# Feed-forward weights: two of the four block sums made by accumulating DMAs, the parts of seven blocks in one tile with five buffers

## The chip, the cores and the metric

One core of a Trainium2 chip runs the whole program: TensorE (PE in the profile; its weight loads PEld), VectorE (DVE), ScalarE (ACT), GpSimd (POOL), SyncE (SP), which issues DMAs, and 16 DMA engines. The metric is the time of one execution on the device in microseconds, the median of several runs.

## The reference, cut to what matters

Two layers of a transformer-like trunk on 640 tokens (512 latent, 128 context). Each layer has three token mixers, a merge with an output projection, and a SwiGLU feed-forward block. The change lies in the latter:

```python
D_MODEL = 1024
D_FF = 256 * ((8 * D_MODEL + 3 * 256 - 1) // (3 * 256))      # 2816
...
    x = x + g1 * mix
    h = rms_norm(x, p['norm2']) * (1 + sc2) + sh2
    x = x + g2 * ((jax.nn.silu(h @ p['w_gate']) * (h @ p['w_up'])) @ p['w_down'])
```

Weights and activations are float32.

## The kernel before

A matrix product in float32 is made from float16 halves: `split` (L186 to L189) writes a rounded half on ACT and the remainder on DVE, and `mm3` (L192 to L202) multiplies high by high, low by high and high by low: three matmuls on each 128 x 128 weight tile.

The three feed-forward products are computed on 2 x 2 blocks with seven block products in place of eight, in the manner of Strassen and Winograd: the weight is cut in four blocks, the tokens in two halves of 320 (`HT`), and the depth in two. Each of the seven products needs one weight block or a sum of weight blocks, and one activation block or a sum of those.

`lhs_parts` (L1197 to L1217) prepares a chunk of weights: the DMA (L1203, issued on SP) loads four blocks of 128 x 256 (512 KB) to a raw tile `wf`, which has two buffers; three blocks are split as they are (`wh` and `wl`, or for every other chunk `uh` and `ul`); four sums go to the tile `ls` (L1210; three on POOL by `SUMP`, one on DVE), and these are split to `vh` and `vl`, four buffers. All of it is emitted at high priority. `block` (from L1219) runs the seven products on two chunks (or three rows of them at the end of the last group), copies some of the sums in PSUM out by ACT (`du`, `dp`) and adds others by DVE (`ff_o`, `ff_s`).

`ffn` (from L1268) runs eleven units u per layer. A unit (`gate_up`) is a block for the gate and one for the up weights, of two chunks each. `gate` takes tanh on ACT and a product on DVE; `up` multiplies in place on POOL, three of four quarters (L1307, tile `ff_s`). At the end of a unit `inputs` makes the block sums of the result (`rhs_sums`, L1189 to L1195, tile `ts`, on POOL but for the last unit) and splits them to the seven blocks of `f`. After units 0 to 4, 5 to 8 and 9 to 10 comes `down` with four blocks each. In layer 0 the modulation weights of layer 1 are loaded and multiplied in between. `norm_sums` (L1367) makes the seven activation blocks `xs` of the normed input, and also uses `rhs_sums`.

`wload` (L175) is the loader of the other weights. Its raw tile `wf` and halves `wh`, `wl` lie in the pool `wst`, which lives as long as the program and is shared with `lhs_parts`. Before the feed-forward comes `merge` (L1125), which also uses POOL (tile `mga`), and in which the first weight chunks of the feed-forward are prepared.

The order of instructions on each engine and each DMA queue is fixed when the program is built, by a scheduler that places them by a simulated time line and by priority. Every engine runs its instructions in that order, and an instruction that waits for a semaphore holds those behind it.

## Time and profile before

| | us |
|---|---|
| median of 3 runs | 2723.09 (2720.1 to 2725.29) |
| the profiled execution's own time | 2721.82 |
| its span, first to last instruction | 2719.8 |
| feed-forward of layer 0, about | 905 to 1385 |
| feed-forward of layer 1, about | 2245 to 2705 |

A busy time is the sum of an engine's instructions. Matmuls overlap in the pipeline, so that a busy PE need not run at its peak. "Idle before" is time in which an engine stood, with the instruction that ended the wait. The chain of waits is followed back from the last instruction: at each step to what released it, or to the instruction ahead of it on its engine. The mean granted clock of PE is 0.973 of its full 2.4 GHz.

### The profile page before, as it was taken

What the parts mean: (1) busy time and instruction counts of PE and PEld (TensorE: products, weight loads), DVE (VectorE), ACT (ScalarE), POOL (GpSimd) and SP (SyncE); (2) the same over time, 40 slices, a digit from 0 to 9 for tenths busy, and PEclk for the clock granted to TensorE, in tenths of its full rate; (3) what the DMA queues carried; (4) which work ended last, traced back from release to release, by engine and by line L of the source; (5) the groups of instructions that cost most, each with busy time, mean ns of one, the idle gap of its engine ahead of it and who ended that gap; (6) DMA issues with size and microseconds to landing.
All of it is one profiled execution on the core that took longest, in us unless ns stands there. A gap on an engine that the chain in (4) does not pass through costs nothing.

```text
span 2719.8 us, 52951 instructions
## 1 busy us (share of the span) xinstructions
PE 2495.5 (92%) x21022; PEld 1613.9 (59%) x21022; DVE 1810.2 (67%) x2966; ACT 1295.5 (48%) x2466; POOL 1093.1 (40%) x1012
## 2 busy tenths in 40 slices
PE   5999999999998899999889989999989988889896
PEld 3656666566345656656566666665653565656574
DVE  5749854325756778878787497442277657888887
ACT  5532754444642544444465346554545444444444
POOL 3252111111137567565533632011112565766764
PEclk9999999999998999999989999999999999999998
DMA  7787564436434164432243965543462621222222
GB/s 295 225 260 233 151 195 124 126 123 202 114 131 157 61 206 131 162 117 89 73 137 106 264 184 161 163 122 119 126 205 74 210 78 40 78 78 78 78 82 67
DMA packets 249400, 382.50 MB, mean 141 GB/s; under 512 B 109824, under 2 KB 155968, under 8 KB 249152
## 3 DMA queue, kind: packets, MB, share of 16 engines
q1 hardware_dynamic: 249152, 379.12, 45.0%
q8 instruction: 165, 2.70, 0.4%
q14 instruction: 83, 0.68, 0.1%
HBM read 291.30 MB, written 73.92 MB: 134 GB/s over the span
## 4 chain that ended last, share of the span: by engine, by line
PE 44%; DVE 18%; POOL 14%; DMA 12%; issue 5%; ACT 5%; SPq 2%; DVEq 0%; POOLq 0%; ACTq 0%
PE f L195 12%; PE g L195 8%; POOL ls L1210 8%; PE ao L872 5%; PE s L195 5%; DMA wf<-in_w_gu 3%; POOL ts L1191 3%; DMA wf<-in_w_down 2%; DVE wl L183 2%; POOL ff_s L1307 1%; DVE vl L189 1%; DVE wl L189 1%; DVE ul L189 1%; DVE z L671 1%; ACT wh L188 1%
## 5 line engine op out<-in xcount | busy, mean ns | idle before, releaser
L195 PEld LDWEIGHTS <-wh 128*128 128x128 f16 x5760 | 560.1, 99 | 250.8 <-issue 34.8
L195 PEld LDWEIGHTS <-wl 128*128 128x128 f16 x2880 | 285.6, 99 | 176.9 <-issue 70.8
L195 PE MATMUL s<-xs,vh 128*128 128x320 f16 x1408 | 308.2, 302 | 25.3 <-ACT du L213 10.7
L195 PEld LDWEIGHTS <-vh 128*128 128x128 f16 x2112 | 209.9, 100 | 92.1 <-issue 5.3
L195 PE MATMUL f<-hh,wh 128*128 128x320 f16 x896 | 251.1, 302 | 1.7 <-ACT st L213 1.6
L195 PE MATMUL f<-hh,wl 128*128 128x320 f16 x896 | 251.2, 301 | 0.0
L1210 POOL TENSOR_TENSOR ls<-wf 128x256 f32<-128x256 f32 (+1 forms) x136 | 137.3, 1014 | 203.7 <-DVE vl L189 188.4
L875 POOL TENSOR_TENSOR pacc<-pe,pacc 128x512 f32<-128x512 f32 x64 | 84.2, 1315 | 325.7 <-ACT pe L213 315.5
L195 PE MATMUL s<-xs,vl 128*128 128x320 f16 x704 | 203.9, 302 | 0.2 <-DVE vl L189 0.2
L195 PE MATMUL g<-hh,wh 128*128 128x320 f16 x704 | 198.7, 304 | 2.8 <-ACT sq L213 1.5
L195 PE MATMUL g<-hh,wl 128*128 128x320 f16 x704 | 198.4, 304 | 0.0
L189 DVE SCALAR_TENSOR_TENSOR vl<-ls,vh 128x1024 f16<-128x1024 f32 (+1 forms) x136 | 185.7, 1389 | 10.8 <-ACT vh L188 10.8
L329 DVE SCALAR_TENSOR_TENSOR wl<-wf,wh 128x512 f16<-128x512 f32 x130 | 89.1, 713 | 137.2 <-ACT wh L213 136.8
L195 PE MATMUL s<-f,vh 128*128 128x320 f16 x704 | 159.9, 310 | 17.1 <-ACT du L213 9.3
L195 PEld LDWEIGHTS <-vl 128*128 128x128 f16 x1056 | 104.8, 99 | 95.8 <-issue 49.2
L183 DVE SCALAR_TENSOR_TENSOR wl<-wf,wh 128x1024 f16<-128x1024 f32 (+4 forms) x116 | 132.6, 1157 | 33.3 <-ACT wh L182 33.0
L188 ACT ACTIVATE vh<-ls 128x1024 f16<-128x1024 f32 (+1 forms) x136 | 133.8, 1020 | 39.4 <-POOL ls L1210 39.3
L195 PE MATMUL f<-hl,wh 128*128 128x320 f16 x896 | 148.7, 299 | 0.0
L195 PE MATMUL s<-xs,wh 128*128 128x320 f16 x528 | 133.6, 306 | 10.0 <-ACT du L213 10.0
L814 POOL TENSOR_TENSOR rc<-rc,rot 128x512 f32<-128x512 f32 (+1 forms) x16 | 27.6, 1724 | 283.3 <-DVE rc L813 266.9
L182 ACT ACTIVATE wh<-wf 128x1024 f16<-128x1024 f32 (+4 forms) x116 | 95.2, 832 | 92.3 <-PE g L195 72.9
L195 PE MATMUL s<-xs,uh 128*128 128x320 f16 x528 | 134.4, 305 | 4.2 <-ACT uh L188 4.2
(382 smaller groups left out, 6202.1 us busy)
## 6 DMA issues: line engine op xcount, KB each, us to landing
wm<-in_w_mod SPq DMA_DIRECT2D x96, 512.0 KB, 4.6
wf<-in_w_gu SPq DMA_DIRECT2D x88, 512.0 KB, 3.6
wf<-in_w_in SPq DMA_DIRECT2D x112, 256.0 KB, 3.5
wf<-in_w_in SPq DMA_DIRECT2D x44, 512.0 KB, 4.0
wf<-in_w_down SPq DMA_DIRECT2D x40, 512.0 KB, 3.6
d_s<-sd SPq DMA_DIRECT2D x20, 768.0 KB, 5.4
d_gate<-st SPq DMA_DIRECT2D x96, 160.0 KB, 3.1
sd<-d_s SPq DMA_DIRECT2D x20, 768.0 KB, 5.7
```

The lines of the kernel that those rows point to most:

```text
L182: nc.scalar.activation(wh, wf, AF.Copy, scale=SW)
L183: nc.vector.scalar_tensor_tensor(wl, wf, SW, wh, op0=ALU.mult, op1=ALU.subtract)
L188: nc.scalar.activation(hi, src, AF.Copy, scale=scale)
L189: nc.vector.scalar_tensor_tensor(lo, src, scale, hi, op0=ALU.mult, op1=ALU.subtract)
L195: mm = lambda *a, **k: nc.tensor.matmul(out, *a, skip_group_check=more, **k)
L329: nc.vector.scalar_tensor_tensor(wl[:, sl], wf, SW, wh[:, sl], op0=ALU.mult, op1=ALU.subtract)
L671: nc.vector.tensor_tensor(z[a, j + 1:N, 0:cc], z[a, j + 1:N, 0:cc], wj, op=ALU.subtract)
L814: nc.gpsimd.tensor_tensor(w[:n], w[:n], self.rot[:n, NS:], op=ALU.mult)
L872: nc.tensor.matmul(po[64 * j:64 * j + 64, :], vt(h, kt), es[j], start=n == 0, stop=n == 4)
L875: nc.gpsimd.tensor_tensor(acc[1], es[1], acc[1], op=ALU.add)
L1191: sub = lambda i, x, y: (self.nc.gpsimd if i in pool else self.nc.vector).tensor_tensor(out[:, i], x, y, op=ALU.subtract)
L1210: tt = lambda i, x, y, op: (nc.gpsimd if i in SUMP else nc.vector).tensor_tensor(t[:, i], x, y, op=op)
```

## The change

The weights of a chunk now come as six blocks in HBM, in the order (1,1), (0,1), (0,0), (0,0), (1,1), (1,0) of the 2 x 2 blocks. SP loads the first five into the raw tile `wg` (640 KB, three buffers). A DMA issued on POOL then adds the sixth block to both of the last two, on their way into the tile (128 KB read as a broadcast, 256 KB written): these are two of the four sums. The third sum is made by DVE, the fourth by POOL, both in place in `wg`. The signs are chosen such that one row of the result comes out negative; that is put right in the scales of `gate`, of the f split, of `norm_sums` and of the modulation (a second `gscale`). The first three blocks are split as they are, the last four after the sums, all to one tile of seven blocks for each half (`pw0`, `pw1`, five buffers). The tables AT7 and BT7 say which slot holds the block of which product.

`rhs_sums` forms the activation sums with the signs that belong to it, in the order 0, 3, 1, 2, and the f split takes three of them together and the fourth by itself, where it was two and two. In `norm_sums` the fourth sum is split by itself too. The pools of `wload` are now opened for each layer: the halves (`wst`) are closed before the merge, the raw tiles (`wf`) before the feed-forward.

```diff
-NSUM = (2,)
+NSUM = (1,)
-SUMP = (0, 1, 3)
+AT7 = {4: 0, 2: 1, 1: 2, 3: 3, 6: 4, 7: 5, 5: 6}
+BT7 = {1: 0, 2: 1, 3: 2, 5: 3, 7: 4, 4: 5, 6: 6}
+WGB = 3
+PWB = 5
...
     def rhs_sums(self, out, b, pool=(0, 1, 2, 3)):
-        sub = lambda i, x, y: (self.nc.gpsimd if i in pool else self.nc.vector).tensor_tensor(out[:, i], x, y, op=ALU.subtract)
-        sub(0, b[:, 0], b[:, 1])
-        sub(1, b[:, 3], out[:, 0])
-        sub(2, b[:, 3], b[:, 0])
-        sub(3, b[:, 2], out[:, 1])
+        tt = lambda i, x, y, op: (self.nc.gpsimd if i in pool else self.nc.vector).tensor_tensor(out[:, i], x, y, op=op)
+        tt(0, b[:, 1], b[:, 0], ALU.subtract)
+        tt(3, b[:, 3], out[:, 0], ALU.add)
+        tt(1, b[:, 3], b[:, 0], ALU.subtract)
+        tt(2, out[:, 3], b[:, 2], ALU.subtract)
-    def lhs_parts(self, pool, src, n, c):
+    def lhs(self, pool, src, n):
+        tile = lambda tag, bufs, dt, q: self.sb(pool, [128, q * 256], tag, dt, bufs)[:, :q * 128 * n].rearrange("p (q x) -> p q x", q=q)
         with self.tc.high_priority():
-            a, t = wide(self.wp, "wf", F32, 2), wide(pool, "ls", F32, 2)
-            nc.sync.dma_start(a, src)
...
-            self.split(w[0], w[1], a[:, 1:4], SW)
-            tt = lambda i, x, y, op: (nc.gpsimd if i in SUMP else nc.vector).tensor_tensor(t[:, i], x, y, op=op)
-            tt(0, a[:, 0], a[:, 3], ALU.add)
-            tt(1, t[:, 0], a[:, 1], ALU.subtract)
-            tt(2, a[:, 1], a[:, 0], ALU.subtract)
-            tt(3, a[:, 2], t[:, 1], ALU.subtract)
-            self.split(v[0], v[1], t, SW)
+            a = tile("wg", WGB, F32, 5)
+            out = [tile(f"pw{i}", PWB, F16, 7) for i in range(2)]
+            nc.sync.dma_start(a, src[:, 0:5])
+            nc.gpsimd.dma_start(a[:, 3:5], src[:, 5:6].to_broadcast([128, 2, 128 * n]), accum_op=ALU.add)
+            self.split(out[0][:, 0:3], out[1][:, 0:3], a[:, 0:3], SW)
+            nc.vector.tensor_tensor(a[:, 2], a[:, 4], a[:, 2], op=ALU.add)
+            nc.gpsimd.tensor_tensor(a[:, 1], a[:, 2], a[:, 1], op=ALU.add)
+            self.split(out[0][:, 3:7], out[1][:, 3:7], a[:, 1:5], SW)
...
-                self.act(t, c, AF.Tanh, scale=0.5 * DS)
+                self.act(t, c, AF.Tanh, scale=(-0.5 if i > 1 else 0.5) * DS)
...
-            for a, b in ((0, 2), (2, 4)):
-                self.split(f[0][:, 3 + a:3 + b], f[1][:, 3 + a:3 + b], t[:, a:b], 0.5 * DS * DS * SF)
+            self.split(f[0][:, 3:6], f[1][:, 3:6], t[:, 0:3], 0.5 * DS * DS * SF)
+            self.split(f[0][:, 6], f[1][:, 6], t[:, 3], -0.5 * DS * DS * SF)
...
-                    parts(3, 7, ts)
+                    parts(3, 6, ts[:, 0:3])
+                    parts(6, 7, ts[:, 3:4], neg=True)
...
+        self.wp = self.pool(wfs, f"wf{l}", 2)
+        self.wq = self.pool(ws, f"wst{l}", 3)
...
+        ws.close()
         wr = self.pool(ys, f"wr{l}", 4, "right")
         self.modscale(l, 1)
         self.gscale(l, 16, DS)
         self.gscale(l, 40, 1.0 / (SW * SF))
+        self.gscale(l, 41, -1.0 / (SW * SF))
...
+        wfs.close()
         with ExitStack() as es:
             self.ffn(l, es, ExitStack())
```

## Rows read from the trace of the kernel before

**Rows 1.** The page: span, then busy time, share and instructions of each engine
```profile
span 2719.8 us, 52951 instructions
...
PE 2495.5 (92%) x21022; PEld 1613.9 (59%) x21022; DVE 1810.2 (67%) x2966; ACT 1295.5 (48%) x2466; POOL 1093.1 (40%) x1012
```

**Rows 2.** Windows: stretch, length, busy us per engine (instructions), granted clock, DMA share, GB/s
```profile
905.00:1385.00 480.00, 433.79 (x3246) 285.51 (x3243) 382.67 (x531) 213.74 (x356) 287.85 (x291) 0.97 0.39 127
2245.00:2705.00 460.00, 405.04 (x2822) 278.84 (x2820) 373.39 (x501) 207.60 (x346) 289.23 (x288) 0.96 0.22 68
...
2501.56:2529.84 28.28, 23.76 (x172) 16.53 (x170) 22.76 (x27) 12.92 (x21) 20.53 (x20) 1.00 0.23 75
...
2448.88:2460.47 11.59, 11.59 (x88) 8.32 (x87) 10.60 (x17) 5.40 (x9) 5.75 (x7) 1.00 0.32 93
```

**Rows 3.** Timeline of PE: start, length, engine, line, operation, count
```profile
2427.46 0.30 PE L195 MATMUL s<-f,vl 128*128 128x320 f16 x1
...
2428.28 0.30 PE L195 MATMUL s<-f,vl 128*128 128x320 f16 x1
```

**Rows 4.** Timeline of POOL in layer 0: first and last of four bursts ts
```profile
1151.76 3.52 POOL L1191 TENSOR_TENSOR ts<-ff_s 128x320 f32<-128x320 f32 x2
...
1242.02 3.54 POOL L1191 TENSOR_TENSOR ts<-ff_s 128x320 f32<-128x320 f32 x2
```

**Rows 5.** Chain of waits through one unit: start, length, what
```profile
2501.56 3.61 DMA wf<-in_w_gu
...
2508.43 1.72 POOL ff_s L1307
...
2510.22 1.78 POOL ts L1191 x2
...
2520.80 2.10 POOL ls L1210 x2
...
2522.92 4.75 DMA wf<-in_w_gu
...
2529.84 3.65 DMA wf<-in_w_down
```

**Rows 6.** Groups by shape, 2270 to 2690 us: busy us, mean ns, idle before
```profile
L189 DVE SCALAR_TENSOR_TENSOR vl<-ls,vh 128x1024 f16<-128x1024 f32 x59 | 81.4, 1398 | 2.7 <-ACT vh L188 2.7
...
L1210 POOL TENSOR_TENSOR ls<-wf 128x256 f32<-128x256 f32 x58 | 59.9, 1036 | 105.3 <-DVE vl L189 101.1 <-DMA wf<-in_w_down 3.1 <-DVE ls L1210 0.9
L188 ACT ACTIVATE vh<-ls 128x1024 f16<-128x1024 f32 x59 | 59.6, 1044 | 9.7 <-POOL ls L1210 9.6
L1210 POOL TENSOR_TENSOR ls<-ls,wf 128x256 f32<-128x256 f32 x58 | 57.3, 991 | 2.0
L1210 POOL TENSOR_TENSOR ls<-wf,ls 128x256 f32<-128x256 f32 x57 | 51.0, 900 | 2.0
...
L1210 DVE TENSOR_TENSOR ls<-wf 128x256 f32<-128x256 f32 x58 | 48.5, 858 | 0.3 <-DMA wf<-in_w_gu 0.2
```

**Rows 7.** The weight loads' line: issue time on SP, ns min/median/max
```profile
L1203 SPq DMA_DIRECT2D wf<-in_w_gu x88: 327/328/333, 821.1 to 2626.6; - x88
```

**Rows 8.** Tile ls over the span: ns min/median/max of the second split
```profile
L189 DVE SCALAR_TENSOR_TENSOR vl<-ls,vh x136: 678/1219/1892, 838.6 to 2695.5; 128x1024 f16<-128x1024 f32 x128, 128x512 f16<-128x512 f32 x8
```

**Rows 9.** DMA issues: count, KB each, median us to landing
```profile
wf<-in_w_gu SPq DMA_DIRECT2D x88, 512.0 KB, 3.6
...
sd<-d_kq SPq DMA_DIRECT2D x40, 256.0 KB, 5.2
...
wf<-in_w_down SPq DMA_DIRECT2D x8, 256.0 KB, 2.7
```

**Rows 10.** Timelines of SP and PE from layer 0 to layer 1
```profile
1368.64 0.89 SPq L181 DMA_DIRECT2D wf<-in_w_tm  x2
...
1382.31 0.30 PE L195 MATMUL s<-f,vh 128*128 128x320 f16 x1
...
1387.24 0.34 PE L195 MATMUL g<-wh,hh 128*128 128x192 f16 x2 [0.49 <-ACT hh L213]
```

More of the change, by code (lines that the diff above doesn't have):

```diff
@@ L136, in __init__ @@
         self.cp = pool("const", 1)
-        self.wp = pool("wst", 3)
         self.tp = pool("tmp", 2)
@@ L176, in wload @@
         nc = self.nc
[L177 to L179 removed]
+        wf = self.sb(raw, [128, n], "wf") if raw else self.sb(self.wp, [128, n], "wf")
+        wh = self.sb(pool or self.wq, [128, n], "wh", F16)
+        wl = self.sb(pool or self.wq, [128, n], "wl", F16)
         with self.tc.high_priority():
@@ L1216, in lhs_parts @@
-        pick = lambda x, q: [x[i][:, q] for i in range(2)]
-        return {1: pick(w, 0), 2: pick(w, 1), 4: pick(w, 2), 5: pick(v, 0), 6: pick(v, 1), 7: pick(v, 2), 3: pick(v, 3)}
+            a = tile("wg", WGB, F32, 5)
[3 more added lines that the diff above has]
+            self.split(out[0][:, 0:3], out[1][:, 0:3], a[:, 0:3], SW)
@@ L1219, in block @@
+            nc.vector.tensor_tensor(a[:, 2], a[:, 4], a[:, 2], op=ALU.add)
+            nc.gpsimd.tensor_tensor(a[:, 1], a[:, 2], a[:, 1], op=ALU.add)
+            self.split(out[0][:, 3:7], out[1][:, 3:7], a[:, 1:5], SW)
+        return {q: [[out[i][:, j, 128 * k:128 * k + 128] for k in range(n)] for i in range(2)] for q, j in AT7.items()}
     def block(self, pool, chunks, rhs, dst, done, urgent=False, after=None):
@@ L1312, in gate_up @@
                     next(mods, None)
-                chunks = [(self.lhs_parts(wp, self.a["w_gu"][l, u, g, c], 256, c), 2 * c, 2) for c in range(2)]
+                chunks = []
+                for c in range(2):
+                    chunks.append((self.lhs(wp, self.a["w_gu"][l, u, g, c], 2), 2 * c, 2))
                 blocks.append(self.block(fa, chunks, lambda q, i, k: xs[q][i][k], dst, done, after=(lambda: inputs(u, s)) if g else None))
@@ L1347, in down @@
                     n = min(2, us[-1] + 1 - u)
-                    src = self.a["w_down"][l, m // 2][:, 512 * u:512 * (u + n)].rearrange("p (q n) -> p q n", q=4)
-                    chunks.append((self.lhs_parts(wp, src, 128 * n, len(chunks)), u, n))
-                run(self.block(fa, chunks, lambda q, i, k: fs_[k][i][:, at7[q]], lambda i: self.sb(fa, [128, HT], "ff_o", bufs=3), done,
+                    chunks.append((self.lhs(wp, self.a["w_down"][l, m // 2][:, 768 * u:768 * (u + n)].rearrange("p (q x) -> p q x", q=6), n), u, n))
+                run(self.block(fa, chunks, lambda q, i, k: fs_[k][i][:, BT7[q]], lambda i: self.sb(fa, [128, HT], "ff_o", bufs=3), done,
                                last and m == KD - 2))
@@ L1387, in norm_sums, with parts @@
                             self.act(c, c, AF.Identity, scale=A, bias=sh)
-                def parts(a, b, src, eng=nc.vector):
+                def parts(a, b, src, eng=nc.vector, neg=False):
                     hi, lo = (xs[i][j][:, a:b, cs] for i in range(2))
-                    self.act(hi, src, AF.Copy)
-                    eng.tensor_tensor(lo, src, hi, op=ALU.subtract)
+                    if neg:
+                        self.split(hi, lo, src, -1.0)
+                    else:
+                        self.act(hi, src, AF.Copy)
+                        eng.tensor_tensor(lo, src, hi, op=ALU.subtract)
                 if h == 0:
@@ L1398, in norm_sums @@
                     parts(2, 3, nt[j][:, 3:4, cs], nc.gpsimd)
-                    parts(3, 7, ts)
-        return {q: [[xs[i][j][:, n] for j in range(4)] for i in range(2)] for n, q in enumerate((1, 2, 3, 5, 6, 7, 4))}
+                    parts(3, 6, ts[:, 0:3])
+                    parts(6, 7, ts[:, 3:4], neg=True)
+        return {q: [[xs[i][j][:, n] for j in range(4)] for i in range(2)] for q, n in BT7.items()}
     def final(self):
@@ L1576, in layout @@
     gu = gu.transpose(0, 7, 1, 3, 5, 6, 2, 4, 8)
-    quads = lambda w: np.stack([w[..., 1, 0, :, :], w[..., 0, 0, :, :], w[..., 0, 1, :, :], w[..., 1, 1, :, :]], -3)
-    r["w_gu"] = quads(gu).reshape(L, NF // 2, 2, 2, 128, 4, 256)
-    dn = f("w_down").reshape(L, 2, NF // 2, 128, 4, 2, 128).transpose(0, 4, 3, 5, 1, 2, 6)
-    dn = quads(dn)
+    six = lambda w: np.stack([w[..., i, j, :, :] for i, j in ((1, 1), (0, 1), (0, 0), (0, 0), (1, 1), (1, 0))], -3)
+    r["w_gu"] = six(gu).reshape(L, NF // 2, 2, 2, 128, 6, 256)
+    dn = six(f("w_down").reshape(L, 2, NF // 2, 128, 4, 2, 128).transpose(0, 4, 3, 5, 1, 2, 6))
     r["w_down"] = cat([dn[..., u:u + 2, :].reshape(L, 4, 128, -1) for u in range(0, NF // 2, 2)], -1)
```

16 lines of the change are left out of this document (3 added, 13 removed).

## The prediction

> **What bounds the kernel now.** I read the page first: PE is busy 92% of 2719.8 us [rows 1], which looks like a kernel bound by its matmuls. The table of windows says otherwise for the feed-forward stages, the only ones in which the change alters much. They run at about 905 to 1385 us (layer 0) and 2245 to 2705 us (layer 1), 940 us together [rows 2]. Matmuls there start about 0.136 us apart when nothing holds them: six steps lie between 2427.46 and 2428.28 [rows 3]. A block on two chunks is 7 products x 2 chunks x 2 x 3 = 84 matmuls, 11.4 us at that pace. One gate-and-up unit u is two blocks, so 22.9 us. The window of one unit is 28.28 us long and holds 172 matmul records; a block without the work at the end of a unit needs 11.59 us, nearly the pace of PE [rows 2]. So in each unit PE stands still for some 5.4 us, and blocks alone are fine. In layer 0, where the modulations of the next layer are mixed in, the three units between the sums at 1151.76 and 1242.02 take 30.1 us each [rows 4].
>
> Why a unit is late is in the chain of waits over that same window [rows 5]. It runs: a weight load, the split on ACT and DVE, the up product on POOL (ff_s), the sums ts, then the sums ls of the weights, which are queued among ff_s and ts, then the next load, which could not start before (a load issued at 2501.56, the next on the chain at 2522.92, the one after at 2529.84). The reason is the raw tile wf: it has two buffers, and the last reader is a POOL sum. A burst on POOL therefore holds the loads, and the split weights reach PE late. DVE is busy 22.76 of the 28.28 us and POOL 20.53 [rows 2], so neither is full, but DVE has little room: it would be the next bound at almost the time that PE needs.
>
> **What leaves POOL and what comes.** There are 136 chunks. Per chunk three POOL sums of 1.04, 0.99 and 0.90 us [rows 6] become one, so 1.95 us leave, 7.8 us in a unit of four chunks. In their place POOL issues one accumulating DMA per chunk. No DMA leaves POOL's queue in the trace of before, so its price there is unknown. Its lower bound is the 0.33 us that SP spends on an issue [rows 7], its upper one the 1.95 us which it replaces; I take 1.0, between the two, since an engine that computes must make the list of rows. Then POOL's work in a unit falls from 20.5 to 16.7 us. DVE keeps one sum (0.86 us) and both splits. It may gain: the second split takes 1.40 us on average in layer 1 and 1.22 at the median [rows 6, 8], and the long ones lie beside POOL's sums. I leave this out of the sum, as DVE does not decide a unit.
>
> **The new cycle of a raw buffer.** Three raw buffers wg replace two wf, and five tiles of parts (2.5 blocks) replace three plus two of wh/uh and four of vh. So the question is what time a wg buffer needs from one load to the next, divided by three.
> - Load: 256 KB land in 2.7 us and 512 KB in 3.6 [rows 9], 0.9 for each 256 KB, so 640 KB take 4.05.
> - Issue on POOL: 1.0.
> - The accumulating transfer writes 256 KB. Lower bound 2.7, a plain load of that size; upper bound 5.4, that load twice, as the destination is read too (the slow 256 KB row has 5.2 [rows 9]). I take 3.3, nearer to the plain load, because the broadcast source is only 128 KB. The first split lies beside it.
> - DVE sum 0.86, POOL sum 0.95, ACT 1.04, DVE 1.40 [rows 6].
>
> That is 12.6 us with no waiting. Now the waits. Before, a wf buffer needs 3.6 for the load and 3.8 for four sums, 7.4 us in all, but its cycle is half a unit, 14.1 us: 6.7 us of waiting in the queues. In a block without the burst it is 11.6, so 4.2. The new cycle is passed on by POOL twice, but POOL is lighter. I take 6 us with the burst and 4.4 without. The cycle is then 18.6 us, over three buffers 6.2 us per chunk and 24.8 us per unit; without the burst 17.0, so 11.3 per block, where PE's own 11.4 decides and nothing changes. A microsecond more or less in the cycle is worth 1.33 us per unit.
>
> So a unit falls from 28.3 to 24.8 us. Ten units per layer (the first is prepared during the merge) give 35 us in layer 1. In layer 0 I take 3.0 us per unit, as the modulation's matmuls fill part of its 30.1 us: 30 us. Together 65 us.
>
> **The other edits.**
> - norm_sums: the last split becomes two on ACT and two on DVE, 8 times per layer. The extra DVE operation is smaller than the 0.86 us sum [rows 6]; all 16 on the path would be 13.7 us, none 0. I take 3, as that stretch waits in turn on ACT, DVE and POOL.
> - The raw and half tiles of wload now live per layer, and the next layer's lie where the f tiles were. Today layer 1's first loads are issued at 1368.64 while the feed-forward ends, and the first product of that layer runs at 1387.24 [rows 10]. If they must wait for the last product on f (about 1382), a load of 2.7 to 3.6 us and its split come later: between 0 and 6 us, once; I take 3.
> - SP: the same number of loads, each a quarter larger. Behind a load that waits for its buffer on SP stand the next weights, in layer 0 the loads of the modulations, and the stores d_x at the end. They wait today in the same way.
> - POOL: the issue waits for its load to land. Behind it are ts, ff_s, the sum of the next chunk and, in the merge, mga; the splits of f on ACT and the second split wait for those. POOL's idle 7.8 us of a unit cover it; what it costs without is the first rival.
> - rhs_sums has as many sums. The f split now needs all four sums first; f is read only by the later down blocks, which hide this, except at the last unit, where one split, about a microsecond, could show. In the merge two sums leave POOL for an issue, which about cancels. The turned signs ride on scales that exist, and one small DVE scale per layer is new: nothing.
>
> **Sum.** The profiled execution took 2721.8 us. Minus 65, plus 6, gives 2662.8; the median of the runs shown is 2723.1, 1.3 above it, so 2664.
>
> **The rivals.**
> POOL's queue blocks (slower). If the scheduler puts an issue right behind its load in time, POOL stands up to the whole 4.05 us and everything behind it too. POOL then needs 16.7 + 4 x 4.05 = 32.9 us per unit, 4.6 more than 28.3; 20 units give 92. A block without burst has 5.75 us of POOL work [rows 2], less 3.9 plus 2.0 plus 8.1 is 12.0 against 11.6, another 10 over 24 blocks. With the 6 us of the other edits the time is 2721.8 + 108 + 1.3, about 2831. It decides from a mean wait of 2.9 us, (28.3 - 16.7) / 4. For: four waits per unit on an engine that runs in order. Against: today POOL's sums follow the same loads and wait little.
>
> The round trip is too long (slower). Its point is a cycle of 21.2 us (28.3 x 3 / 4), so an issue and transfer of 6.9 us together with my waits. If the transfer reads twice over, in two passes of 5.2 us [rows 9], the cycle is 18.6 - 3.3 + 10.4 = 25.7, a unit 34.3 us: 20 x 6.0 = 120, and blocks without burst 16.1 against 11.6, 24 x 4.5 = 108; some 2957. At the milder 5.4 us the unit is 27.6 us and the blocks 12.7, and the sum comes out about 2741. The Trainium skill, in "Collectives: The Full Stack" (The bandwidth ceiling), says that an add inside a DMA is slow because it reads two sources, which halves the rate, not because of the adding. By it the transfer would be at my upper bound of 5.4; no row of before shows an add in a DMA.
>
> PE decides (faster still): with the short bounds (0.33 and 2.7) the cycle is 17.3, 23.1 us per unit, almost PE's 22.9. Then 52 in layer 1 and 45 in layer 0: 2632.
>
> Nothing is gained: the burst ff_s, ts stays in front of the second split's sum, or DVE at 22.8 us keeps its order, and a unit stays at 28. Time 2715 to 2730. For: POOL still stands twice in the cycle. Against: raw and split weights for four blocks can be in store in place of three, and the burst takes POOL less than one block's time.
>
> **How the numbers follow.** Forecast 0.42 (2640 to 2700), PE decides 0.14, nothing gained 0.12, POOL blocked 0.19, long trip 0.13. A measurement tells 0.2%, 5.4 us, from no change. Faster 0.42 + 0.14 + 0.04 of "nothing" = 0.60; same 0.08; slower 0.32. Both signs hold much, so the range reaches from 2610, below the PE case by its unknowns, into the blocked and long cases up to 2790, leaving about 0.04 below and 0.14 above; the likeliest case alone has 2640 to 2700.
>
> **What would show it.** A unit in layer 1 (distance between ts bursts) near 25 us, blocks without burst at 11.4 to 11.7; POOL issues of about 1 us; 256 KB accumulating in 3 to 4 us; POOL waiting for wg under 2 us each. Wrong: POOL waits for wg of 3 us or more (first rival), splits on ACT waiting for the accumulated tile with POOL idle (second), or a unit still near 28 with DVE idle for POOL (fourth).

## The result and the profile after

The changed kernel takes 2750.35 us (2745.9 to 2755.07), the kernel before on the same chip 2724.19 us. The ratio is 1.0098, 95% interval 1.0074 to 1.0122: 1% slower, where I forecast 2664. Its profiled execution took 2747.1 us, 2745.2 of them span.

The page of the changed kernel, first its engines (as [rows 1]) and its software queue, then three groups and three DMA issues with their landings (as [rows 6] and [rows 9]):

```profile
PE 2503.0 (91%) x21022; PEld 1606.3 (59%) x21022; DVE 1739.1 (63%) x2984; ACT 1308.2 (48%) x2482; POOL 941.4 (34%) x876
...
q0 software_dynamic: 36992, 34.61, 8.8%
...
L192 ACT ACTIVATE pw<-wg 128x1024 f16<-128x1024 f32 (+3 forms) x272 | 247.7, 923 | 251.4 <-POOL wg L1213 157.7
...
L1210 POOL DMA_DIRECT2D wg<-in_w_gu x88 | 105.6, 1205 | 218.9 <-DMA wg<-in_w_gu 120.3
...
L1212 DVE TENSOR_TENSOR wg<-wg 128x256 f32<-128x256 f32 (+1 forms) x136 | 91.8, 680 | 87.6 <-DMA wg<-in_w_gu 61.5
...
wg<-in_w_gu SPq DMA_DIRECT2D x88, 640.0 KB, 4.9
...
wg<-in_w_down SPq DMA_DIRECT2D x40, 640.0 KB, 4.1
...
wg<-in_w_gu POOLq DMA_DIRECT2D x88, 256.0 KB, 4.6
```

POOL lost 152 us of work, as meant, and DVE 71. But POOL now stands for its load before an issue, DVE for the accumulating transfer before its sum, and ACT for POOL before the second split. Windows of two units in layer 1 (as [rows 2]; their ends are the starts of ts bursts):

```profile
2514.62:2542.88 28.26, 24.48 (x164) 16.16 (x163) 18.64 (x26) 13.22 (x20) 15.31 (x15) 0.94 0.56 131
2542.88:2571.70 28.82, 25.94 (x185) 17.31 (x183) 23.14 (x29) 13.65 (x22) 16.86 (x16) 1.00 0.58 129
```

A unit is as long as before, 28.3 and 28.8 us (28.3 in [rows 2]). POOL has 15 to 17 us of work in it instead of 20.5 and the DMA engines are busy 0.56 to 0.58 of the time instead of 0.23. The chain of waits through the first of these units (start, length, what), to be laid beside [rows 5]:

```profile
2521.18 4.90 DMA wg<-in_w_gu
...
2526.64 4.37 DMA wg<-in_w_gu
...
2531.10 0.06 DVE wg L1212
...
2531.93 1.55 DVE pw L193
...
2535.04 5.10 DMA wg<-in_w_gu
...
2540.71 1.20 POOL wg L1210
```

Before, POOL's sums of weights stood between two loads. Now two transfers stand there, one behind the other: a load of 4.90 us and then, from 2526.64, the accumulating transfer of 4.37.

Where the 25.4 us of the span went is read from the first and last matmul of each stage, from the start of one to the start of the other, in one execution of each kernel. In us; "L1 mixers" are the products on hh, the merge runs from the first product on the mixers' results (yh) to the last one with w_out, FFN are the products on xs and f; the kernels are those of the experiments below:

| kernel | L0 merge | L0 FFN | L1 mixers | L1 merge | L1 FFN | span |
|---|---|---|---|---|---|---|
| before | 123.6 | 468.6 | 580.8 | 122.2 | 453.6 | 2719.8 |
| after | 129.2 | 470.5 | 589.3 | 128.9 | 447.5 | 2745.2 |
| e1_no_acc | 120.7 | 440.6 | 590.7 | 121.0 | 411.5 | 2659.1 |
| e3_pool_waits | 121.2 | 440.7 | 593.3 | 120.8 | 414.4 | 2672.1 |
| e2_plain | 123.2 | 456.0 | 589.9 | 123.9 | 436.2 | 2705.0 |
| e13_two_loads | 129.1 | 457.0 | 585.2 | 127.6 | 429.9 | 2712.5 |
| e17_other_order | 122.3 | 474.4 | 585.1 | 125.5 | 453.3 | 2735.4 |
| e8_engine_sums | 125.4 | 468.4 | 590.7 | 125.5 | 449.5 | 2737.2 |
| e4_wgb4 | 127.9 | 471.9 | 581.4 | 127.0 | 446.3 | 2734.4 |
| e4c_wgb4_pwb5 | 111.0 | 457.7 | 577.7 | 110.0 | 438.4 | 2718.3 |
| e11_behind | 109.8 | 453.6 | 588.0 | 109.3 | 439.6 | 2723.1 |
| e5_pools | 124.2 | 469.3 | 584.2 | 124.1 | 456.5 | 2733.6 |
| e6_late | 124.2 | 469.7 | 588.4 | 124.4 | 451.4 | 2738.6 |
| e10_fft1 | 128.5 | 473.1 | 590.0 | 128.8 | 448.8 | 2745.8 |
| e14_two_loads_late | 125.4 | 456.8 | 588.9 | 124.2 | 427.9 | 2700.9 |
| e15_dve_sums | 124.7 | 460.8 | 585.6 | 123.0 | 433.3 | 2703.7 |
| e16_two_loads_4 | 108.4 | 448.5 | 581.5 | 108.3 | 427.7 | 2695.5 |

From before to after: FFN −4 us where I had −65, the merges +12 where I had 0, the mixers of layer 1 +8.5 where I had nothing, and +9 over the rest (mostly layer 0's mixers +3.0 and the two attention stages +5.0; one stage of one execution moves by some 3 us on its own, see the experiment on the pools).

### The profile page after: what moved, and what is told of

It reads as the page before. It is cut to its first block, busy times and chain, and to the rows that moved or that the text cites. A ratio compares the mean times of both kernels' runs of the same rounds, so it can differ in the third digit from the quotient of the medians.

```text
span 2745.2 us, 53163 instructions
## 1 busy us (share of the span) xinstructions
PE 2503.0 (91%) x21022; PEld 1606.3 (59%) x21022; DVE 1739.1 (63%) x2984; ACT 1308.2 (48%) x2482; POOL 941.4 (34%) x876
## 3 DMA queue, kind: packets, MB, share of 16 engines
q0 software_dynamic: 36992, 34.61, 8.8%
## 4 chain that ended last, share of the span: by engine, by line
PE 44%; DVE 19%; DMA 18%; issue 6%; ACT 6%; POOL 5%; SPq 2%; POOLq 0%; DVEq 0%; ACTq 0%
PE f L199 11%; PE s L199 9%; PE g L199 7%; DMA wg<-in_w_gu 6%; PE ao L876 4%; DVE pw L193 4%; DMA wg<-in_w_down 2%; DVE z L675 2%; ACT pw L192 1%; DVE wl L187 1%; DVE zw L673 1%; POOL wg L1213 1%; DMA d_s<-sd 1%; DVE wg L1212 1%; PE at L980 1%
## 5 line engine op out<-in xcount | busy, mean ns | idle before, releaser
L199 PEld LDWEIGHTS <-pw 128*128 128x128 f16 x5544 | 539.7, 99 | 347.3 <-issue 55.5
L199 PEld LDWEIGHTS <-wh 128*128 128x128 f16 x4944 | 477.6, 99 | 211.5 <-issue 29.7
L199 PE MATMUL s<-xs,pw 128*128 128x320 f16 x3696 | 541.2, 304 | 47.2 <-ACT pw L192 13.3
L192 ACT ACTIVATE pw<-wg 128x1024 f16<-128x1024 f32 (+3 forms) x272 | 247.7, 923 | 251.4 <-POOL wg L1213 157.7
L193 DVE SCALAR_TENSOR_TENSOR pw<-wg,pw 128x1024 f16<-128x1024 f32 (+3 forms) x272 | 314.8, 1171 | 72.8 <-ACT pw L192 71.9
L199 PE MATMUL s<-f,pw 128*128 128x320 f16 x1848 | 273.6, 303 | 35.6 <-ACT pw L192 17.1
L1210 POOL DMA_DIRECT2D wg<-in_w_gu x88 | 105.6, 1205 | 218.9 <-DMA wg<-in_w_gu 120.3
L1213 POOL TENSOR_TENSOR wg<-wg 128x256 f32<-128x256 f32 (+1 forms) x136 | 125.0, 924 | 66.2 <-DVE wg L1212 63.8
L1212 DVE TENSOR_TENSOR wg<-wg 128x256 f32<-128x256 f32 (+1 forms) x136 | 91.8, 680 | 87.6 <-DMA wg<-in_w_gu 61.5
L199 PE MATMUL g<-hl,wh 128*128 128x320 f16 x704 | 114.6, 300 | 0.0
```

The costliest lines, as they stand in the source:

```text
L192: nc.scalar.activation(hi, src, AF.Copy, scale=scale)
L193: nc.vector.scalar_tensor_tensor(lo, src, scale, hi, op0=ALU.mult, op1=ALU.subtract)
L199: mm = lambda *a, **k: nc.tensor.matmul(out, *a, skip_group_check=more, **k)
L1210: nc.gpsimd.dma_start(a[:, 3:5], src[:, 5:6].to_broadcast([128, 2, 128 * n]), accum_op=ALU.add)
L1212: nc.vector.tensor_tensor(a[:, 2], a[:, 4], a[:, 2], op=ALU.add)
L1213: nc.gpsimd.tensor_tensor(a[:, 1], a[:, 2], a[:, 1], op=ALU.add)
```

## The experiments

Each kernel is the changed one with the edit shown; medians are of its own runs, the kernel before, run beside them, gave 2719 to 2722. Theory A, which I began with: the time of a raw buffer's round trip (load, accumulating transfer, sums, second split) sets the pace. Theory B: POOL's queue does, because the issue waits for its load. Theory M: the pools cost time in the merge.

### What the accumulating transfer costs

Without the transfer:

```diff
-            nc.gpsimd.dma_start(a[:, 3:5], src[:, 5:6].to_broadcast([128, 2, 128 * n]), accum_op=ALU.add)
```

> The changed kernel without the accumulating DMA: the sixth weight block is never added, so two of the seven block sums are incomplete; all other work stays. Theory A (the way of a raw buffer from load to load, 21.2 us over three buffers, sets the 28 us of a unit): some 6 us leave the way, a unit falls to 22.9 to 25 us, each feed-forward stage by 35 to 50 us, the whole to 2660 to 2690. Theory B (POOL held at the head of its queue by the DMA's wait for the load) expects the same here. Theory C (the order of ff_s, ts, splits and sums sets the unit, whoever makes the sums): the unit stays at 27 to 28.5 us and the whole at 2735 to 2750. Theory M (the early weight loads crowd out the merge's loads) expects the first product with w_out in layer 0 still near 860 us, against 841.8 before.

2665.18 us, ratio 0.9801 (0.9784 to 0.9817). 85 us hang on this one line; of these the table has 66 in the FFN stages and 16 in the merges. Two windows of a unit, and the landing of the loads:

```profile
2469.00:2494.10 25.10, 23.25 (x170) 16.18 (x168) 21.10 (x27) 13.62 (x22) 12.08 (x11) 1.00 0.34 106
2494.10:2519.20 25.10, 23.20 (x171) 16.30 (x169) 20.71 (x27) 12.96 (x20) 11.84 (x12) 1.00 0.32 105
...
wg<-in_w_gu SPq DMA_DIRECT2D x88, 640.0 KB, 5.0
```

PE is busy 23.2 of 25.1 us, so a unit is now nearly its matmuls. The loads land no sooner without the transfers (5.0 us, with them 4.9), so it is not by slowing the loads that the transfers cost. It could still be POOL's issue and its wait. So POOL's wait stays and only the transfer goes: a tiny sum of eight columns a block stands in POOL's queue in the transfer's place and waits for the same load.

```diff
-            nc.gpsimd.dma_start(a[:, 3:5], src[:, 5:6].to_broadcast([128, 2, 128 * n]), accum_op=ALU.add)
+            nc.gpsimd.tensor_tensor(a[:, 3:5, 0:8], a[:, 0:2, 0:8], a[:, 3:5, 0:8], op=ALU.add)
```

> The accumulating DMA is replaced by an addition of 2 x 8 columns on POOL in place, which waits for the load as the DMA's issue did, and stands where it stood; the sixth block is never added. Theory A: the transfer's 4.6 us are gone from the way, so the unit falls nearly as far as without the DMA, to 23.5 to 25.5 us, the whole to 2665 to 2700. Theory B: POOL is still held until the load lands, so the unit stays near 28 us and the whole at 2730 to 2750. Theory C: as B.

2670.84 us, 0.9815 (0.98 to 0.983). Its group on the page:

```profile
L1210 POOL TENSOR_TENSOR wg<-wg 128x16 f32<-128x16 f32 x136 | 65.0, 478 | 332.3 <-DMA wg<-in_w_gu 169.0
```

POOL stands 169 us for the loads of w_gu, more than the 120.3 of the changed kernel, and the kernel is within 6 us of the one without the wait. Theory B falls: standing at the head of POOL's queue is not what costs; the transfer's trip is, its landing together with an issue that holds POOL for 1.2 us where this sum takes 0.48.

The third cut leaves the transfer and takes away only its addition:

```diff
-            nc.gpsimd.dma_start(a[:, 3:5], src[:, 5:6].to_broadcast([128, 2, 128 * n]), accum_op=ALU.add)
+            nc.gpsimd.dma_start(a[:, 3:5], src[:, 5:6].to_broadcast([128, 2, 128 * n]))
```

> The changed kernel with the same transfers from POOL, which write the sixth block over the last two and add nothing: two block sums are left out. Theory A1 (the add makes the transfer slow, as it reads its target too): the 256 KB land in 2.7 to 3.3 us in place of 4.6, the way of a raw buffer shortens by 1.5 us and a unit by some 2 us, the whole to 2700 to 2720. Theory A2 (POOL's issue and a transfer behind a load are slow, with or without an add): landing in 4.2 to 4.7 us and the whole at 2740 to 2755.

2708.13 us, 0.9961 (0.9946 to 0.9976). Its page:

```profile
q0 software_dynamic: 10624, 34.61, 3.9%
...
L1210 POOL DMA_DIRECT2D wg<-in_w_gu x88 | 64.4, 732 | 231.9 <-DMA wg<-in_w_gu 165.9
...
wg<-in_w_gu POOLq DMA_DIRECT2D x88, 256.0 KB, 3.2
```

The addition makes 36,992 packets out of 10,624 for the same 34.61 MB, takes 8.8% of the DMA engines' time instead of 3.9%, 1.2 us of POOL for an issue instead of 0.73, and a landing of 4.6 us instead of 3.2. In the whole: half of the 85 us (2750 to 2708) is the addition, the other half (2708 to 2665) the transfer as such.

### More buffers instead of a shorter trip

If the trip sets the pace, one more raw buffer should hide it. The first kernel has four raw buffers and gives up one of the five buffers of parts; the second keeps all five and gives up one of the two tanh tiles.

```diff
-WGB = 3
-PWB = 5
+WGB = 4
+PWB = 4
```

> Four raw buffers wg in place of three, four tiles of parts in place of five (there is no room for both). Theory A: a way of 21.2 us over four buffers is 5.3 us per chunk, under PE's 5.7, so the unit falls to 23 to 25 us and the whole to 2670 to 2705. Theory B: loads start earlier, so POOL is held less; a fall of 1 to 2 us per unit, the whole 2705 to 2730. Theory C: the unit stays at 28, the whole at 2740 to 2755. Theory M: one more load goes ahead of the merge's, so the merges get no earlier.

2732.36 us, 1.0032 (1.0019 to 1.0046); units of about 27.5 us, not 23 to 25.

```diff
-WGB = 3
+WGB = 4
-                t = self.sb(fa, [128, HT], "ff_t", bufs=2)
+                t = self.sb(fa, [128, HT], "ff_t", bufs=1)
```

> Four raw buffers and five tiles of parts; the room comes from ff_t, one buffer in place of two. Theory A' (two rings: three raw buffers need 20 us for three chunks, and a parts tile is held for some 10.5 us before PE may use it and about 16 by PE, 26 us over four or five tiles): neither ring binds any more (20 over 4 is 5.0, 26 over 5 is 5.3 us, both under PE's 5.7), so a unit falls to 23.5 to 25.5 us and the whole to 2675 to 2705. Rival (a transfer gets slower the more are under way, so a further buffer gives little): the unit stays at 27 to 28, the whole 2720 to 2740.

2724.49 us, 1.0018 (1.0005 to 1.0032); units of 28.4, 28.1 and 26.9 us. The tanh tile alone, as a control:

> Computes all. The changed kernel (2750) with one buffer of the tanh tile instead of two and nothing else: the control for the two kernels with four raw buffers, which gave that buffer up for room. If the tanh buffer costs nothing, 2745 to 2755, and the fourth raw buffer (2724.5, with units of 27.7 us instead of 28) is worth what those kernels showed. If it holds PE up at the ends of blocks (a tanh and a product of 1 to 1.5 us, four a gate block): units of 29 to 31 us, 2760 to 2790, and the fourth raw buffer is worth more than it showed.

2748.06 us, 1.0094 (1.0073 to 1.0115): one tanh tile costs nothing. So A, put as "cycle divided by buffers", missed twice. The 26 us of the fourth buffer come in part from elsewhere: the first loads of w_gu are issued late, at 851.56 instead of 796.17, the merges shrink to 110 us, and 27.7 us pass between the last product on w_out and the first on xs, where the changed kernel has 4.4. Over both layers the merges lose 37 us, the waits behind them gain 46 and the FFN loses 22: 13 us in all. Another 11.6 come from the mixers of layer 1, of which more below.

I then thought that the written order was to blame: each engine comes to a chunk's sums so early that it must stand there, however many buffers there are. The next kernel puts a chunk's load, transfer and first split ahead of the sums of the chunk before, on four raw buffers and one tanh tile:

```diff
-    def lhs(self, pool, src, n):
+    def lhs_begin(self, pool, src, n):
...
+    def lhs_end(self, chunk, behind):
...
+            s = nc.vector.tensor_tensor(a[:, 2], a[:, 4], a[:, 2], op=ALU.add)
+            if behind is not None:
+                self.after(s.ins, behind)
...
+        this, self.ahead = self.ahead, self.lhs_begin(pool, *self.todo.pop(0)) if self.todo else None
+        return self.lhs_end(this, self.ahead and self.ahead[3])
```

> Computes all. Four raw buffers, five buffers of parts, one of the tanh tile (to make room), and the order is changed: each chunk's load, accumulating transfer and first split are put ahead of the chunk before's two sums and second split, and on DVE the sum stands behind the next chunk's first split. So no engine comes to a chunk's sums until the chunk after it has been loaded, and the accumulating transfer has a chunk's time (some 6 us) more before anyone stands waiting for it. To be read against the kernel with four raw buffers and five of parts in the old order (2724.5, units of 27.7 us). Theory D (the order brings the engines to the sums too soon, so they stand waiting at the heads of their queues): units of 24.5 to 26 us in layer 1, whole 2680 to 2705. Rival T (the raw buffers' cycle decides, not the order): the cycle is longer by the same chunk's time, so units stay at 27 to 28.5, whole 2715 to 2745. Rival U: one tanh buffer holds ACT and PE up, units over 28.5, over 2745.

2724.96 us, 1.0021 (1.0008 to 1.0035), units of 27.2, 27.9 and 26.6 us: what the fourth buffer gives without it. What DVE's sum of a chunk waits for says more. Its row in the old order with four buffers (e4c), to be laid beside the one of the changed kernel above:

```profile
L1212 DVE TENSOR_TENSOR wg<-wg 128x256 f32<-128x256 f32 (+1 forms) x136 | 90.9, 696 | 10.3 <-DMA wg<-in_w_gu 10.2
```

With three buffers DVE stands 87.6 us before these sums, with four 10.3 in the old order and 2.9 in the new one; ACT still waits 80.0 us for POOL's sum in layer 1. So with four buffers it is no longer the transfer that DVE waits for, something behind it holds a chunk back, and the order I tried did not mend it. POOL still stands 94.7 us for the loads of w_gu in e4c; in e16 below, with the load in two pieces, it is 67.9 us and the units are 25 to 26 us. Whether that stand is what holds the chunks was not tried by itself.

### The same transfer, begun sooner

The accumulating transfer needs blocks 3 and 4 of five. Loading these first, by themselves, lets it start after 256 KB instead of 640:

```diff
-            nc.sync.dma_start(a, src[:, 0:5])
+            nc.sync.dma_start(a[:, 3:5], src[:, 3:5])
+            nc.sync.dma_start(a[:, 0:3], src[:, 0:3])
```

> Computes all. The load of five blocks is two loads: blocks 3 and 4 (256 KB), which the accumulating transfer needs, and behind them blocks 0 to 2 (384 KB). So the accumulating transfer can start when 256 KB have landed instead of 640 KB (4.9 us in the changed kernel's trace). Theory D (what costs is the time from a load's issue to the landing of the accumulating transfer, at some 30 us of the whole per us of it, by the runs without the add, 2708, and without the transfer, 2665 to 2671, against 2750): the accumulating transfer starts 1 to 2 us sooner, minus one more issue on SP; the whole 2700 to 2735. Rival R (the transfers share a bandwidth and the sum of the bytes decides, so that the order of the blocks changes nothing): 2745 to 2755. Rival S (more packets and issues make the landings longer): over 2755.

2708.99 us, 0.9966 (0.9951 to 0.9981): 41 us off, and faster than before. The control has the same two loads in the other order:

> Computes all. The control for the kernel with two loads (2709): the same two loads in the other order, blocks 0 to 2 first and blocks 3 and 4 behind them, so that the accumulating transfer starts no sooner than in the changed kernel, while the first split may start sooner. Theory D (the start of the accumulating transfer decides): the gain of 41 us goes, 2738 to 2760. Rival Z (two smaller loads are better than one, whichever comes first, or the first split's earlier start decides): 2705 to 2725.

2737.19 us, 1.0056 (1.0033 to 1.008), a microsecond below what theory D allowed. So 28 of the 41 us are the order, and at most 13 the splitting. By stages the order counts for more: the FFN takes 886.9 us with blocks 3 and 4 first, 927.7 in the other order and 918.0 in the changed kernel. What the control gains on the changed kernel is not there but in the merges (10 us) and the mixers of layer 1 (4 us). The landings of the two, that of the blocks-3-and-4-first kernel in the first fence:

```profile
wg<-in_w_gu SPq DMA_DIRECT2D x88, 384.0 KB, 4.0
...
wg<-in_w_gu SPq DMA_DIRECT2D x88, 256.0 KB, 3.1
wg<-in_w_gu POOLq DMA_DIRECT2D x88, 256.0 KB, 5.5
```

```profile
wg<-in_w_gu SPq DMA_DIRECT2D x88, 384.0 KB, 4.0
...
wg<-in_w_gu SPq DMA_DIRECT2D x88, 256.0 KB, 4.5
wg<-in_w_gu POOLq DMA_DIRECT2D x88, 256.0 KB, 4.6
```

The transfer takes 5.5 us beside the 384 KB load, but what it needs has landed after 3.1 us instead of 4.9: load and transfer together 8.6 us, against 9.5 in the changed kernel. In the control they take 4.5 and 4.6, and the load is issued 0.4 us behind the other one: 9.5 again. Windows of two units of the kernel with blocks 3 and 4 first:

```profile
2488.40:2513.80 25.40, 24.17 (x176) 16.88 (x175) 21.95 (x28) 14.07 (x22) 16.23 (x15) 1.00 0.59 144
2513.80:2539.90 26.10, 24.94 (x180) 17.14 (x179) 22.12 (x27) 12.78 (x20) 16.25 (x16) 1.00 0.60 143
```

Units of 25.4 and 26.1 us, with the same DMA share of 0.6 as the changed kernel (the control has 0.54 to 0.56 and units of 27.6 to 29.0). So it is not the DMA engines' load that decides, but what comes first. That 0.9 us is worth 28 is more per microsecond than the addition showed (1.4 us of landing and 0.5 of issue, 42 us); what POOL's shorter wait for its load adds here (62.8 us for w_gu, 97.6 in the control) was not tried by itself.

The opposite: no transfer at all, four blocks loaded, and both sums on POOL in place, so the layout and buffers are the change's and the work is nearly that of before:

```diff
-            nc.sync.dma_start(a, src[:, 0:5])
-            nc.gpsimd.dma_start(a[:, 3:5], src[:, 5:6].to_broadcast([128, 2, 128 * n]), accum_op=ALU.add)
+            nc.sync.dma_start(a[:, 0:4], src)
+            nc.gpsimd.tensor_tensor(a[:, 4], a[:, 0], a[:, 3], op=ALU.add)
+            nc.gpsimd.tensor_tensor(a[:, 3], a[:, 2], a[:, 3], op=ALU.add)
```

> The change without its DMA: four distinct blocks are loaded (512 KB) and the two sums are made by two more POOL sums in place, so POOL makes three sums as before; three raw buffers, five tiles of parts, signs and pools stay. The result is the reference's. Theory A: the way of a raw buffer loses load, issue and transfer (some 10 us) for 3.6 and two sums of about 1 us; a unit falls to 24 to 26 us in spite of POOL's burst, the whole to 2680 to 2710. Rival (POOL's burst of three sums per chunk sets the unit, as in the kernel before): the unit stays at 27.5 to 28.5, the whole 2720 to 2745.

2737.42 us, 1.0067 (1.0052 to 1.0082), units of 27.3 to 27.8 us. The rival was right, and theory A missed once more: on the same three buffers the load (4.2 us) and two sums (0.96 and 1.07) take 4.5 us less than load, issue and transfer, and the units gain less than one. So POOL's sums cost as much as the transfer that replaced them, which is why the FFN came out even (917.9 us here, 918.0 in the changed kernel): the change took the burst away and put a wait of the same price in its place.

### The pools and the merge

The kernel before, with nothing of the change but the places of its pools:

```diff
-        self.wp = pool("wst", 3)
...
-            a, t = wide(self.wp, "wf", F32, 2), wide(pool, "ls", F32, 2)
+            a, t = wide(pool, "wf", F32, 2), wide(pool, "ls", F32, 2)
...
+        self.wp = self.pool(wfs, f"wf{l}", 2)
+        self.wq = self.pool(ws, f"wst{l}", 3)
```

> The kernel before, with the change's pools alone: raw tiles and halves of the other weights per layer, closed before the merge and the feed-forward, and the feed-forward's raw tiles (two, of 512 KB) in a pool of their own. Sums and splits are as before. Theory M: the feed-forward's loads no longer stand behind those of w_out for a shared raw buffer, go ahead of the merge's loads, and the merges end later: 10 to 25 us over both layers, the whole 2732 to 2750, with the units at 28.3 us as before. Rival: the pools cost nothing, the merge is held by POOL's issues and the DMA's traffic: 2719 to 2728.

2737.96 us, 1.0058 (1.0037 to 1.0079): 16 us for a change that adds no work. Not in the merges, as M had it (124.2 and 124.1 us, 2.5 us more in all). The largest single piece, 3.4 of the 13.8 us between the two spans, is in the mixers of layer 1. The diff moves only the pools of their weights, but the planner now lays their instructions in another order. The other pieces lie in all stages and are under 3 us each; their cause is open. How the order differs is seen on POOL, before:

```profile
1674.66 1.27 POOL L814 TENSOR_TENSOR rc<-rc,rot 128x512 f32<-128x512 f32 x1 [10.39 <-DVE rc L813]
1678.66 1.54 POOL L736 TENSOR_TENSOR S<-S,cs 128x512 f32<-128x512 f32 x1 [2.74 <-PE ao L831]
1692.11 1.71 POOL L814 TENSOR_TENSOR rc<-rc,rot 128x512 f32<-128x512 f32 x1 [11.91 <-DVE rc L813]
```

and at the same place of the changed kernel (13.3 us later, as the layer begins later):

```profile
1677.76 1.80 POOL L818 TENSOR_TENSOR rc<-rc,rot 128x512 f32<-128x512 f32 x1 [13.04 <-DVE rc L817]
1692.22 1.41 POOL L740 TENSOR_TENSOR S<-S,cs 128x512 f32<-128x512 f32 x1 [12.66 <-DMA S<-in_st]
1694.12 1.71 POOL L818 TENSOR_TENSOR rc<-rc,rot 128x512 f32<-128x512 f32 x1 [0.49 <-DVE rc L817]
1710.18 1.04 POOL L740 TENSOR_TENSOR S<-S,cs 128x512 f32<-128x512 f32 x1 [14.34 <-DVE S L759]
1713.33 1.71 POOL L818 TENSOR_TENSOR rc<-rc,rot 128x512 f32<-128x512 f32 x1 [2.11 <-DVE rc L817]
```

Before, the rc at 1674.66 stands ahead of S. After, S, for whose load POOL stands 12.66 us, comes first, and that rc runs at 1694.12: 6.2 us later than before, with the 13.3 us taken off.

Of 549 ACT instructions of that stretch, compared by the names of their tiles, none is displaced in the three kernels with four raw buffers and the old order of chunks, and they take 577.7 to 581.5 us (before: 580.8). In e14 and e15 81 are, 588.9 and 585.6; in e5, e13 and e17 145, 584.2 to 585.2; in the changed kernel and seven others some 226, 588.0 to 593.3. In layer 0 the order is the same in all, and the same stretch there takes 599.6 to 606.0, a spread of 6.4 us that the order does not explain. So another order goes with 3 to 12 us more there; I did not set the order alone, so this is an agreement over 17 kernels, not an experiment of its own.

The merge is another matter. There the first unit's loads are issued ahead of the merge's own. SP of the changed kernel:

```profile
796.17 0.37 SPq L1209 DMA_DIRECT2D wg<-in_w_gu  x1
...
797.11 0.38 SPq L1209 DMA_DIRECT2D wg<-in_w_gu  x1
...
798.10 1.32 SPq L1209 DMA_DIRECT2D wg<-in_w_gu  x1
...
809.37 2.42 SPq L185 DMA_DIRECT2D wf<-in_w_br  x2
```

Before, w_br is loaded from 794.50 on and the first w_gu at 821.10. With three raw buffers free from the start, the first three chunks go first, and their accumulating transfers behind them. The window from 800 to 850 us, before and then after (the merge begins at 785.6 and at 791.3):

```profile
800.00:850.00 50.00, 41.73 (x284) 28.65 (x282) 46.52 (x54) 19.30 (x26) 45.76 (x37) 0.94 0.64 224
```

```profile
800.00:850.00 50.00, 33.73 (x226) 22.78 (x225) 39.56 (x47) 17.84 (x24) 31.41 (x29) 0.86 0.93 288
```

The DMA share is 0.93 instead of 0.64, PE has done 226 matmuls instead of 284, and its granted clock is 0.86 instead of 0.94. It is not the later start of the merge: with windows moved by it, 794.30 to 844.30 before and 805.70 to 855.70 after, the share is 0.93 instead of 0.73, the matmuls 240 instead of 310 and the clock 0.86 instead of 0.97. Taking the priority from the first unit's chunks:

```diff
-        with self.tc.high_priority():
+        with self.tc.high_priority() if urgent else ExitStack():
...
-                    chunks.append((self.lhs(wp, self.a["w_gu"][l, u, g, c], 2), 2 * c, 2))
+                    chunks.append((self.lhs(wp, self.a["w_gu"][l, u, g, c], 2, u > 0), 2 * c, 2))
```

> The changed kernel, but the weights of each layer's first unit are prepared without high priority, so their loads, adding DMAs and sums should stand behind the merge's own work. Theory M' (in the merges the early loads and adding DMAs crowd the DMA engines and hold POOL; each merge takes 5.5 to 6.7 us longer than before for that): from the first product of the merge to the last with w_out 119 to 125 us in both layers, against 129 now, the whole 2732 to 2745. Rival: what the merge gains the first unit loses, as its weights then come late; 2745 to 2760.

2737.97 us, 1.0063 (1.0041 to 1.0085), merges of 124 us: 9 of the 12 us of the merges are these chunks' place. Without the transfer (e1) the merges are 121 us at the old priority, so it is the loads with their transfers that crowd them, not the loads alone. But the control e17 has both at the old priority, and merges of 122.3 and 125.5 us, so when the transfers come counts too; how they hold the merge was not tried further.

### Kernels that beat both

The two loads and the late first unit:

> Computes all. The kernel with the two loads (blocks 3 and 4 first), and the first unit's weights of each layer without high priority, so that they don't come ahead of the merge's own loads (which alone gave 2738 against 2750, merges of 124 us instead of 129). If the two effects are separate they add: 12 us under the kernel with two loads alone, 2690 to 2723 by theory D, 2733 to 2743 by rival R. If the late first unit loses in the first wait what the merge gains: the same as two loads alone.

2705.71 us, 0.9943 (0.9922 to 0.9963). The merges are 4 us shorter each, as expected, but the whole gains only 3 of these, which the runs (2698.6 to 2709.0, against 2702.7 to 2717.5) hardly tell from nothing.

The same with POOL's last sum on DVE (one word: gpsimd becomes vector):

> Computes all. The kernel with the two loads and the late first unit (2706), and the last sum of a chunk is DVE's instead of POOL's, so that nothing lies between DVE's two sums. In the parts' chain it takes away the hop to POOL and the wait for POOL's queue (in the kernel with two loads 1.7 us from the start of DVE's sum to that of POOL's, then 1.1 to the second split; DVE's sum is 0.67 us). Theory D (each us of the chain from the load's issue to the second split is worth some 25 us of the whole): the chain is 1 to 1.5 us shorter, so 2665 to 2690. Rival V (DVE's queue is what the second split waits in; 0.67 us more of DVE per chunk puts it later): 2700 to 2725. Rival W (PE or the groups before the merge decide by now): 2695 to 2706.

2713.68 us, 0.9961 (0.9942 to 0.9979). Theory D is wrong here, and the time lies in rival V's range: the hop to POOL is gone, and ACT waits for DVE's sum as long as it waited for POOL's (65.7 us instead of 55.6 in layer 1). A microsecond is not worth the same wherever it lies in the trip.

The two loads and four raw buffers, with one tanh tile:

> Computes all. The kernel with the two loads (2709), with four raw buffers instead of three and one tanh buffer (which costs nothing: 2748 against 2750). A fourth raw buffer brought 26 us to the changed kernel (2724.5) though its feed-forward stages grew (485 and 466 us against 475 and 452, the first unit late) and its merges shrank (111 and 110 us against 129). Theory D with the fourth buffer as slack for the transfer's latency: the gains add in part, 2680 to 2700. Rival X (the fourth buffer's gain is that of the merges alone, at the price of a later first unit): merges of 110 to 114 us, units of 26 to 27.5 us, 2695 to 2712. Rival Y (the two loads already give what the fourth buffer gave): 2705 to 2720.

2701.71 us, 0.9931 (0.9911 to 0.9952), units of 25.6, 25.8 and 24.9 us. It has the lowest median of those that compute all, 0.7% under the kernel before, though its interval overlaps that of the two loads with the late first unit (0.9922 to 0.9963). The time fits rival X, the merges and units are shorter than X had them; its merges are 108 us, with 27 us behind each until the first product on xs, and its layer 1 has the order of before.

## Why the prediction was wrong

**The bound was right in part.** POOL's burst made a unit late: with nothing in its place (e1) the units are 24 to 26 us and the FFN stages 70 us shorter (922.2 to 852.1), where my sum had 65 and 24.8. That it does so by holding raw buffers is not shown, and more buffers did not help: e8 has the burst on three buffers in place of two, and its units are still 27.3 to 27.8 us.

**What leaves POOL: right.** I put POOL's work in a unit at 16.7 us, and it is 15.3 and 16.9. The issue, bounded by 0.33 and 1.95 and taken at 1.0, takes 1.2.

**The cycle of a raw buffer: the step that failed, by its sizes.** I had 12.6 us without waiting. Measured: load 4.9 (I had 4.05), issue 1.2 (1.0), transfer 4.6 (3.3), DVE's sum 0.68 (0.86), POOL's 0.97 (0.95), ACT 1.05 (1.04), DVE 1.42 (1.40); together 14.8. With my own 6 us of waiting this is 20.8, times 4/3 a unit of 27.7, where 28.3 and 28.8 were measured. So the sum itself, with the right sizes, would have said that the FFN gains next to nothing. The larger mistake was to take the accumulating transfer near a plain load because its source is small: without the addition it lands in 3.2 us (e2), with it in 4.6. The load I read off a line through 256 and 512 KB. It is not longer because the accumulating transfers keep the DMA engines busier (share 0.57, before 0.23): without them, at 0.32 to 0.34, it takes 5.0 us (e1). Why it takes 4.9 is open.

**The formula failed too.** "Cycle over buffers" says 20.8 us per unit for a fourth raw buffer, so PE's pace, and 26.1 to 29.3 were measured in layer 1 after the first unit (e4, e4c). By it the kernel without the addition has units of 25.2 us (cycle 12.9 + 6), and 25.3 to 29.2 were measured there. By it the kernel with POOL's sums in place of the transfer (e8, cycle 10.3 + 6) runs at PE's pace, and its units are 27.3 to 27.8. So that it fits the changed kernel once the sizes are right is in part luck. The 6 us of waiting are not a constant: they are what the queues of ACT, DVE and POOL make of the rest.

**The other edits.** The weights of the next layer do wait for the end of the FFN, as I feared: the first load of layer 1 is issued at 1395.72, the last product on f starts at about 1395.3. But this cost 0.3 us, not 3 (4.9 us from the last product on f to the first on hh, now 5.2): in between PE has the norm's products, and its first product of the layer waits for hh, not for weights. I had "about cancels" for the merge, by counting POOL's work; it was 12 us, and what I left out is what three free raw buffers let SP send ahead of the merge's own loads, which stand on the same queue. The split of norm_sums (my +3) was not measured by itself. I gave the pools nothing but the transition; their run shows 16 us (e5), 3.4 of them in the mixers of layer 1, where the instructions come in another order. No view of before could show that; what I could have done is to widen the "other edits" for it.

**The rivals.** The round trip that is too long came nearest: at a transfer of 5.4 us I had units of 27.6 and 2741 us, and it is 28.1 (a mean of three) and 2750 with 4.6, the rest of its length being the load and the issue. I had given it 0.13. That the whole time fits is luck: its 2741 has some 26 us for longer blocks without a burst, and the two stretches of four such blocks and a unit take 147.9 us together in layer 1, against 147.1 before; the time was lost in the merges, the mixers and the rest. "POOL's queue blocks" would have decided from a mean wait of 2.9 us; POOL's waits for w_gu are 120.3 us, 3.3 each over the 37 issues that wait (my sign, 3 us or more), but 1.4 over all 88, so its condition was not met, and e3, which stands longer, loses at most 6 us. "PE decides" is nearly what the kernel without the transfer is. "Nothing is gained" had the units (28 us) and the FFN right, but not the reason: the burst of ff_s and ts is in e1 too, and its units are 24 to 26 us.

**The price of the addition.** The Trainium skill, in "Collectives: The Full Stack" (The bandwidth ceiling), says of the reducing step of a ring that its add is slow because of two source reads, at half the rate. The trace agrees for the DMA engines' time: 8.8% of 2745 us against 3.9% of 2705 is 2.3 times as much for the same bytes. The landing grew less, from 3.2 to 4.6 us, 1.44 times.

## What to carry to other kernels

Work that moves from an engine into a DMA moves from busy time into latency: price it as a round trip of a buffer (load, issue, transfer, and each engine that must come by), with the durations that such a transfer shows in a run, and not by the engine's time that it frees. Where a transfer must follow a load, split the load so that what the transfer needs comes first; here that was worth 28 us in 2750. A fourth buffer brought 26 us, half of them in the merges and the FFN, and another order with it nothing. A formula such as cycle over buffers holds no further than the runs that bear it out. And when buffers come free earlier, ask what the queue will send ahead of the stage that is running.

## What the runs showed of the hardware

- An accumulating DMA of 256 KB issued by POOL took 1.2 us of POOL and landed in 4.6 us; the same without the addition 0.73 and 3.2; a plain load of 256 KB by SP 2.7 us before.
- The addition turned 10,624 packets into 36,992 and made the DMA engines busy 2.3 times as long for the same 34.61 MB.
- Beside a load of 384 KB the same accumulating transfer took 5.5 us.
- A load of 640 KB landed in 4.9 us with the accumulating transfers beside it (DMA share 0.56 to 0.58) and in 5.0 without them (0.32 to 0.34).
- The mixers of layer 1 took 577.7 to 581.5 us in the four kernels with one order of instructions and 584.2 to 593.3 in the thirteen with others; those of layer 0 took 599.6 to 606.0 in one and the same order.
